# Matmul, GELU, matmul on one core: loads through SyncE's queue with casts on VectorE, and a transpose by the DMA crossbar

## The chip, the core and the metric

The kernel runs on one core of a Trainium2 chip. The core has five engines with instruction streams of their own: TensorE (PE, matrix products; its weight loads are shown apart as PEld), VectorE (DVE), ScalarE (ACT), GpSimd (POOL) and SyncE (SP, which here only issues DMAs). Sixteen DMA engines move data between HBM and the on-chip memory SBUF; PE writes its results to PSUM. The metric is the time of one execution on the device in microseconds (us); less is better.

## The reference

```
a: (1024, 1024)   b: (1024, 2048)   c: (2048, 1024)   all float32
h   = a @ b
h   = 0.5 * h * (1 + tanh(sqrt(2/pi) * (h + 0.044715 * h**3)))
out = h @ c       (1024, 1024) float32
```

## The kernel before

All products run in bf16 with f32 accumulation. A matmul of PE contracts over the 128 partitions, so the first product needs a transposed: `aT[h]` holds half h of a's rows (512 of them) as 8 slices of k. The first product is computed as the transpose of h: for each of the 16 column tiles t of b (128 columns), 8 matmuls over k give a tile of 128 x 512 in PSUM, ACT applies the GELU and writes it to `hT[h]` as bf16 (L103). The second product takes `hT[h]` as it lies: 8 row tiles by 2 column halves, 16 matmuls each (L171), evacuated by DVE (L163) and stored through SP (L164).

The schedule is manual: each engine runs its instructions in the order of the program. The order of the work is this.

- Opening: SP loads half 0 of a and the first 768 columns of b (six tiles, `N0`) as f32, slice of k by slice (L60, L66). DVE casts a (L91), PE transposes it by products with an identity matrix (L94), DVE copies the result from PSUM (L95), ACT casts b (L97). PE runs the six tiles' matmuls k by k, one slice behind (`mm0`, L86).
- A gate on POOL (L75) reads one column of the sixth slice of b, so that POOL's loads start only when that slice has landed.
- All further loads are issued by POOL's queue, which casts f32 to bf16 on the way: the next 512 columns of b (`N1`, four loads of two k slices, L110), the last 768 columns of b (two groups of 384, `W2`, each in two loads of four k slices, L110 too), the second half of a (`ab1`, four loads of 128 rows, L142), then c (eight loads of two tiles, L137).
- PE runs the four tiles of `N1` (L118), then tiles 10 to 15 of half 0 (`mm1(t, 0)`, L127). After tiles 11 to 14 the function `turn(j)` transposes one of the four row blocks of a's second half: eight PE transposes (L149) into one PSUM tile, one copy by DVE into `aT[1]` (L150). Block j fills columns 128 j to 128 j + 127 of each of the eight slices.
- PE then runs all 16 tiles of half 1 (`mm1(t, 1)`, L127), each of which reads all of `aT[1]`, then the second product.

Of the kernel before, what the change touches and what calls it, by code (L numbers as in the profile page):

```python
# [9 lines left out]
F32 = mybir.dt.float32  # L10
BF16 = mybir.dt.bfloat16
# [5 lines left out]
def kernel(ctx, tc, a, b, c, out):  # L17
    nc = tc.nc
    M, K = a.shape
    _, N = b.shape  # L20
    _, P = c.shape
    KT = K // 128
    NT = N // 128
# [7 lines left out]
    av = a.rearrange("(mt p) k -> p mt k", p=128)  # L31
    bv = b.rearrange("(kt p) n -> p kt n", p=128)
    cv = c.rearrange("(nt p) q -> p nt q", p=128)

    ctx.enter_context(tc.manual_schedule())
    consts = ctx.enter_context(tc.tile_pool(name="consts", bufs=1))
    keep = ctx.enter_context(tc.tile_pool(name="keep", bufs=1))
    astage = ctx.enter_context(tc.tile_pool(name="astage", bufs=4))
    abf = ctx.enter_context(tc.tile_pool(name="abf", bufs=4))
    b0stage = ctx.enter_context(tc.tile_pool(name="b0stage", bufs=8))  # L40
    opool = ctx.enter_context(tc.tile_pool(name="opool", bufs=4))
    ppool = ctx.enter_context(tc.tile_pool(name="ppool", bufs=6, space=PSUM))
    tpool = ctx.enter_context(tc.tile_pool(name="tpool", bufs=2, space=PSUM))
# [3 lines left out]
    ident = consts.tile([128, 128], BF16, name="ident")  # L47
    make_identity(nc, ident)

    aT = [keep.tile([128, KT, H], BF16, name=f"aT{h}") for h in range(2)]  # L50
    b_sb = keep.tile([128, KT, N], BF16, name="b_sb")
    c_sb = keep.tile([128, NT, P], BF16, name="c_sb")
# [3 lines left out]
    a_st, b_st = {}, {}  # L56
# [9 lines left out]
        nc.sync.dma_start(out=st, in_=bv[:, k, 0:W0])  # L66
        b_st[k] = st

    gate = consts.tile([128, 1], F32, name="gate")
    for k, n in ((0, 1), (1, 1), (2, 2), (4, 2), (6, 2)):  # L70
        load_a0(k, n)
        for i in range(n):
            load_b0(k + i)

    nc.gpsimd.tensor_copy(gate, b_st[5][:, 0:1])  # L75
    g = consts.tile([128, 1], F32, name="g")
    nc.scalar.activation(g, warm[:, 0:1], AF.Gelu_apprx_tanh)
    wps = tpool.tile([128, H], F32, name="pt")
# [10 lines left out]
    for k in range(KT):  # L89
        ab = abf.tile([128, 4, 128], BF16, name="ab")  # L90
        nc.vector.tensor_copy(ab, a_st[k])  # L91
        pt = tpool.tile([128, H], BF16, name="pt")
# [14 lines left out]


    def load_b(k0, kn, n0, w):
        nc.gpsimd.dma_start(out=b_sb[:, k0:k0 + kn, ds(n0, w)], in_=bv[:, k0:k0 + kn, ds(n0, w)])  # L110

    ps = [(tpool if t < 2 else ppool).tile([128, H], F32, name="pt" if t < 2 else "ps")
          for t in range(N1)]
    for k in range(0, KT, 2):
        load_b(k, 2, W0, W1)
        for i in range(2):
            for t in range(N1):
                nc.tensor.matmul(ps[t], b_sb[:, k + i, ds(W0 + t * 128, 128)], aT[0][:, k + i, :],  # L118
                                 start=(k + i == 0), stop=(k + i == KT - 1))
# [4 lines left out]
    def mm1(t, h):  # L124
        p = ppool.tile([128, H], F32, name="ps")
        for k in range(KT):
            nc.tensor.matmul(p, b_sb[:, k, ts(t, 128)], aT[h][:, k, :],  # L127
                             start=(k == 0), stop=(k == KT - 1))
        gelu(t, h, p)

    W2 = 384
    for n0 in range(W0 + W1, N, W2):
        for k in range(0, KT, 4):
            load_b(k, 4, n0, W2)

    def load_c(t0):
        nc.gpsimd.dma_start(out=c_sb[:, t0:t0 + 2, :], in_=cv[:, t0:t0 + 2, :])  # L137

    a1 = []
    for j in range(4):  # L140
        st = abf.tile([128, K], BF16, name="ab1")
        nc.gpsimd.dma_start(out=st, in_=av[:, 4 + j, :])  # L142
        a1.append(st)

    def turn(j):
        ab = a1[j]
        pt = tpool.tile([128, KT, 128], BF16, name="pt")
        for k in range(KT):
            nc.tensor.transpose(pt[:, k, :], ab[:, ts(k, 128)], ident)  # L149
        nc.vector.tensor_copy(aT[1][:, :, ts(j, 128)], pt)  # L150

    for t in range(N0 + N1, NT):
        mm1(t, 0)
        if NT - 5 <= t < NT - 1:
            turn(t - (NT - 5))
    for t in range(0, NT, 2):
        load_c(t)
    for t in range(NT):
        mm1(t, 1)

# [5 lines left out]
    for mt in range(MT):  # L166
        h, j = divmod(mt, 4)
        for q0, w in ((0, 512), (512, 512)) if mt < MT - 1 else ((0, 512), (512, 256), (768, 256)):
            p = ppool.tile([128, w], F32, name="ps", padded_shape=[128, H])
# [34 lines left out]
```

## Time and profile before

| | us |
|---|---|
| three runs | 133.13, 130.68, 131.53 |
| median | 131.53 |
| the profiled execution | 133.13 |
| its span, first to last instruction | 130.9 |

| engine | busy us | share of the span |
|---|---|---|
| PE | 119.2 | 91% |
| PEld | 56.3 | 43% |
| ACT | 27.2 | 21% |
| DVE | 21.0 | 16% |
| POOL | 14.6 | 11% |

The profiled execution is the slowest of the three, 1.2% above the median. In the lines that follow, L127 is line 127 of the kernel; a group "L149 PE MATMUL pt<-ident,ab" is named by its line, engine, operation, output and inputs. In the 40 slices a digit is an engine's busy share of a slice in tenths. A bracket at the end of a line of the timeline gives the idle time of the engine before the instruction and what ended it.

### The profile page before, as it was taken

To read this page: it belongs to the slowest core of one execution; us is meant where nothing else is said; L and a number is where in the kernel's file an instruction comes from. 1 tells how busy PE (TensorE), PEld (TensorE's weight loads), DVE (VectorE), ACT (ScalarE), POOL (GpSimd) and SP (SyncE) were. 2 spreads that over 40 slices of the span, in tenths; PEclk is the share of its full clock that TensorE was granted. 3 is DMA by queue.
4 is the path that set the end of the run, shared out by engine and by line. 5 is a ranking of instruction groups with operands and counts; after the bars stand their busy time and mean duration, and the time that the engine had idled before them with its cause. 6 is when DMAs were issued, how large, how long until landed. Compare 5 with 4: busy or idle time off the path is not lost.

```text
span 130.9 us, 1420 instructions
## 1 busy us (share of the span) xinstructions
PE 119.2 (91%) x591; PEld 56.3 (43%) x602; DVE 21.0 (16%) x38; ACT 27.2 (21%) x50; POOL 14.6 (11%) x27
## 2 busy tenths in 40 slices
PE   6856899998299999999999999999999999999990
PEld 2323444443155444444444444444444444444570
DVE  0223451000042200000000022222222222211121
ACT  4045556516111333333333100000000000000000
POOL 2000099232462000000000000000000000000000
PEclk9999999999999999999999999999999999999999
DMA  3999999999999999950000022221111222222231
GB/s 110 201 367 380 378 236 168 179 202 205 209 211 210 211 212 211 211 112 1 0 0 0 5 80 80 80 78 59 60 59 69 80 80 80 80 80 80 80 120 40
DMA packets 12196, 17.37 MB, mean 133 GB/s; under 512 B 800, under 2 KB 6688, under 8 KB 12192
## 3 DMA queue, kind: packets, MB, share of 16 engines
q0 software_dynamic: 5952, 7.87, 34.8%
q1 hardware_dynamic: 6240, 9.44, 20.8%
q8 instruction: 4, 0.07, 0.2%
HBM read 20.97 MB, written 4.19 MB: 192 GB/s over the span
## 4 chain that ended last, share of the span: by engine, by line
PE 70%; DMA 18%; POOL 5%; SPq 4%; issue 1%; DVE 0%
PE ps L171 42%; PE ps L127 26%; DMA ab<-in_a_dram 10%; DMA b_st<-in_b_dram 7%; POOL b_sb L110 4%; SPq L66 3%; PE pt L149 1%; SPq L60 1%; DVE ot L163 0%; POOL gate L75 0%
## 5 line engine op out<-in xcount | busy, mean ns | idle before, releaser
L171 PE MATMUL ps<-c_sb,hT 128*128 128x512 bf16 (+1 forms) x267 | 55.2, 367 | 0.3
L127 PE MATMUL ps<-aT,b_sb 128*128 128x512 bf16 x172 | 38.8, 379 | 0.6 <-DMA b_sb<-in_b_dram 0.4
L171 PEld LDWEIGHTS <-hT 128*128 128x128 bf16 x272 | 26.6, 98 | 28.9
L127 PEld LDWEIGHTS <-b_sb 128*128 128x128 bf16 x176 | 16.9, 98 | 20.5 <-DMA b_sb<-in_b_dram 0.9
L103 ACT ACTIVATE hT<-ps 128x512 bf16<-128x512 f32 x30 | 17.3, 602 | 30.0 <-PE ps L127 27.7
L163 DVE COPY ot<-ps 128x512 f32<-128x512 f32 (+1 forms) x17 | 11.2, 660 | 73.2 <-PE ps L171 73.2
L86 PE MATMUL ps<-aT,b_sb 128*128 128x512 bf16 x47 | 11.5, 379 | 0.1
L97 ACT ACTIVATE b_sb<-b_st 128x384 bf16<-128x384 f32 x16 | 7.5, 515 | 10.7 <-DMA b_st<-in_b_dram 10.5
L94 PE MATMUL pt<-ident,ab 128*128 128x128 bf16 x32 | 3.4, 233 | 3.9 <-DVE ab L91 3.9
L137 POOL DMA_DIRECT2D c_sb<-in_c_dram x8 | 5.7, 714 | 6.9 <-DMA b_sb<-in_b_dram 4.7
L86 PEld LDWEIGHTS <-b_sb 128*128 128x128 bf16 x48 | 4.4, 98 | 4.0
L150 DVE COPY aT<-pt 128x1024 bf16<-128x1024 bf16 x4 | 2.8, 692 | 20.5 <-PE pt L149 20.5
L110 POOL DMA_DIRECT2D b_sb<-in_b_dram x8 | 6.0, 775 | 0.0
L80 PE MATMUL pt<-warm 128*128 128x512 bf16 x10 | 4.5, 632 | 1.2 <-DVE warm L46 1.2
L94 PEld LDWEIGHTS <-ab 128*128 128x128 bf16 x32 | 2.3, 104 | 6.9 <-DVE ab L91 5.8
L118 PE MATMUL ps<-aT,b_sb 128*128 128x512 bf16 x16 | 4.8, 379 | 0.1
L118 PEld LDWEIGHTS <-b_sb 128*128 128x128 bf16 x32 | 3.1, 98 | 3.8
L91 DVE CAST ab<-a_st 128x512 bf16<-128x512 f32 x8 | 3.6, 445 | 6.2 <-DMA a_st<-in_a_dram 6.2
L118 PE MATMUL pt<-aT,b_sb 128*128 128x512 bf16 x15 | 4.5, 379 | 0.0
L149 PE MATMUL pt<-ident,ab 128*128 128x128 bf16 x32 | 2.5, 220 | 2.3 <-DMA ab<-in_a_dram 2.3
L95 DVE COPY aT<-pt 128x512 bf16<-128x512 bf16 x8 | 3.4, 425 | 6.4 <-PE pt L94 6.4
L149 PEld LDWEIGHTS <-ab 128*128 128x128 bf16 x32 | 2.0, 98 | 3.5 <-DMA ab<-in_a_dram 2.8
(13 smaller groups left out, 7.5 us busy)
## 6 DMA issues: line engine op xcount, KB each, us to landing
c_sb<-in_c_dram POOLq DMA_DIRECT2D x8, 512.0 KB, 15.3
out_dram<-ot SPq DMA_DIRECT2D x15, 256.0 KB, 2.0
b_st<-in_b_dram SPq DMA_DIRECT2D x8, 384.0 KB, 8.7
a_st<-in_a_dram SPq DMA_DIRECT2D x3, 512.0 KB, 8.9
b_sb<-in_b_dram POOLq DMA_DIRECT2D x4, 384.0 KB, 11.4
b_sb<-in_b_dram POOLq DMA_DIRECT2D x4, 256.0 KB, 5.9
ab<-in_a_dram POOLq DMA_DIRECT2D x4, 256.0 KB, 13.8
a_st<-in_a_dram SPq DMA_DIRECT2D x2, 256.0 KB, 4.2
```

The costliest lines, as they stand in the source:

```text
L80: nc.tensor.matmul(wps, warm[:, 0:128], warm, start=True, stop=True)
L86: nc.tensor.matmul(ps[t], b_sb[:, k, ts(t, 128)], aT[0][:, k, :], start=(k == 0), stop=(k == KT - 1))
L94: nc.tensor.transpose(pt[:, ts(j, 128)], ab[:, j, :], ident)
L97: nc.scalar.activation(b_sb[:, k, ts(i, W0 // 2)], b_st[k][:, ts(i, W0 // 2)], AF.Copy)
L103: nc.scalar.activation(hT[h][:, t, :], p, AF.Gelu_apprx_tanh)
L110: nc.gpsimd.dma_start(out=b_sb[:, k0:k0 + kn, ds(n0, w)], in_=bv[:, k0:k0 + kn, ds(n0, w)])
L118: nc.tensor.matmul(ps[t], b_sb[:, k + i, ds(W0 + t * 128, 128)], aT[0][:, k + i, :], start=(k + i == 0), stop=(k + i == KT - 1))
L127: nc.tensor.matmul(p, b_sb[:, k, ts(t, 128)], aT[h][:, k, :], start=(k == 0), stop=(k == KT - 1))
L137: nc.gpsimd.dma_start(out=c_sb[:, t0:t0 + 2, :], in_=cv[:, t0:t0 + 2, :])
L149: nc.tensor.transpose(pt[:, k, :], ab[:, ts(k, 128)], ident)
L163: nc.vector.tensor_copy(ot[:, 0:w], p)
L171: nc.tensor.matmul(p, hT[h][:, t, ts(j, 128)], c_sb[:, t, ds(q0, w)], start=(t == 0), stop=(t == NT - 1))
```

## The change

The loads that POOL issued with a cast are now issued by SP as f32 into staging buffers and cast by DVE. b and c share a new pool `stage` of three buffers of 8 KB per partition; a's second half goes into the four buffers of the opening's pool `astage`. The gate on POOL is gone. `turn(j)` no longer uses PE, PSUM and DVE's copy, but issues one transposing DMA from the bf16 copy `ab1[j]` into the same columns of `aT[1]`. In the program, and so in SP's queue, the four turns stand after all loads of b and a, with the first four loads of c between them (turn, load of c, turn, load of c, and so on), and the other four loads of c after them; all of this stands ahead of `mm1(10, 0)` in the program. The pool of the opening slices of b, `b0stage`, has eight buffers before and after.

```
+    stage = ctx.enter_context(tc.tile_pool(name="stage", bufs=3))
...
-    gate = consts.tile([128, 1], F32, name="gate")
...
-    nc.gpsimd.tensor_copy(gate, b_st[5][:, 0:1])
...
     def load_b(k0, kn, n0, w):
-        nc.gpsimd.dma_start(out=b_sb[:, k0:k0 + kn, ds(n0, w)], in_=bv[:, k0:k0 + kn, ds(n0, w)])
+        st = stage.tile([128, 2048], F32, name="st")
+        sv = st[:, 0:kn * w].rearrange("p (k n) -> p k n", k=kn)
+        nc.sync.dma_start(out=sv, in_=bv[:, k0:k0 + kn, ds(n0, w)])
+        nc.vector.tensor_copy(b_sb[:, k0:k0 + kn, ds(n0, w)], sv)
...
     def load_c(t0):
-        nc.gpsimd.dma_start(out=c_sb[:, t0:t0 + 2, :], in_=cv[:, t0:t0 + 2, :])
+        st = stage.tile([128, 2048], F32, name="st")
+        sv = st.rearrange("p (t q) -> p t q", t=2)
+        nc.sync.dma_start(out=sv, in_=cv[:, t0:t0 + 2, :])
+        nc.vector.tensor_copy(c_sb[:, t0:t0 + 2, :], sv)
 
     a1 = []
     for j in range(4):
-        st = abf.tile([128, K], BF16, name="ab1")
-        nc.gpsimd.dma_start(out=st, in_=av[:, 4 + j, :])
+        st = astage.tile([128, K], F32, name="a_st")
+        nc.sync.dma_start(out=st, in_=av[:, 4 + j, :])
         a1.append(st)
 
+    ab1 = []
+    for j in range(4):
+        ab = abf.tile([128, K], BF16, name="ab1")
+        nc.vector.tensor_copy(ab, a1[j])
+        ab1.append(ab)
+
     def turn(j):
-        ab = a1[j]
-        pt = tpool.tile([128, KT, 128], BF16, name="pt")
-        for k in range(KT):
-            nc.tensor.transpose(pt[:, k, :], ab[:, ts(k, 128)], ident)
-        nc.vector.tensor_copy(aT[1][:, :, ts(j, 128)], pt)
-
+        nc.sync.dma_start_transpose(out=aT[1][:, :, ts(j, 128)], in_=ab1[j])
+
+    for j in range(4):
+        turn(j)
+        load_c(2 * j)
+    for t in range(8, NT, 2):
+        load_c(t)
     for t in range(N0 + N1, NT):
         mm1(t, 0)
-        if NT - 5 <= t < NT - 1:
-            turn(t - (NT - 5))
-    for t in range(0, NT, 2):
-        load_c(t)
     for t in range(NT):
         mm1(t, 1)
```

## The prediction

> **What bounds the kernel now.** I read the 40 slices of the page first, then the chain of work that ended last in order of time, then the waits of PE, then those of SP's queue.
>
> ```profile
> PE   6856899998299999999999999999999999999990
> DMA  3999999999999999950000022221111222222231
> GB/s 110 201 367 380 378 236 168 179 202 205 209 211 210 211 212 211 211 112 1 0 0 0 5 80 80 80 78 59 60 59 69 80 80 80 80 80 80 80 120 40
> ```
>
> A slice is 3.27 us. PE is full from slice 12 to the end; the only thin places are the opening and slice 11. The DMA engines are full for the first 17 slices, some 57 us: all inputs are fetched once, as fast as the engines go. The GB/s fall to about 205 from slice 7 on because POOL's loads are counted after their cast from f32 to bf16; about 410 GB/s were read.
>
> ```profile
> 16.25 5.83 POOL b_sb L110 x8
> 22.09 13.67 DMA ab<-in_a_dram
> 35.76 0.05 issue
> 35.80 0.62 PE pt L149 x8
> 36.43 0.65 PE ps L127 x3
> ...
> 38.15 0.45 PE pt L149 x8
> ...
> 40.33 0.45 PE pt L149 x8
> ...
> 42.50 0.45 PE pt L149 x8
> 42.95 1.08 PE ps L127 x5
> 44.02 0.05 issue
> 44.08 10.74 PE ps L127 x49
> ```
>
> The columns are start and duration in us. Until 35.8 us the chain runs through the loads, POOL's and then that of the second half of a; from there it is PE alone. The eight matmuls of output tile t = 15 of the first half start with the last transposes done and end at 44.5 us (127 x8 at 0.216 each from 42.78). So **the second half's matmuls start at T = 44.5 us**, and what follows T is fixed: 128 matmuls at 0.2155 us (27.6) and 16 groups of 16 (55.5) to 127.6 us. The whole change is judged by what it does to T. Three lines of the timeline show what PE loses before T:
>
> ```profile
> 30.74 2.27 PEld L127 LDWEIGHTS <-b_sb 128*128 128x128 bf16 x12 [0.90 <-DMA b_sb<-in_b_dram]
> 30.75 2.76 PE L127 MATMUL ps<-aT,b_sb 128*128 128x512 bf16 x12 [0.41 <-DMA b_sb<-in_b_dram]
> 35.80 0.62 PE L149 MATMUL pt<-ident,ab 128*128 128x128 bf16 x8 [2.29 <-DMA ab<-in_a_dram]
> ```
>
> It waits 0.4 us for b and 2.3 us for a; the four transpose groups take 0.62 + 3 x 0.45 = 2.0 us. That is 4.7 us, so T cannot fall below 39.8 us.
>
> **What the Trainium skill says.** "DMA: Bandwidth & Descriptors", section "Queues, rings and completion order": all that SP issues goes to one ring on each DMA engine, and a ring's descriptors are consumed in order. The trace agrees: the opening's loads of a, all issued by SP, need 2.6 us to land at the shortest and 9.9 at the longest, and loads of a and b land in the order of issue. "VectorE: DVE Perf Modes", section "The three transpose paths": a 128x128 bf16 transpose takes 1309 ns through the DMA crossbar and 390 on TensorE. The trace has 220 ns for a PE transpose and eight in 0.45 us; it has no crossbar transpose. "TensorE: Matmul & The Clock Gate", section "What's actually happening": after an idle window of about 3.4 us PE runs at half rate until it has been busy for about as long. The trace shows the slow start: the ten warm-up matmuls of L80 take 4.45 us, and the same shape later needs 0.216 each.
>
> **The change, part by part.**
>
> *Loads move from POOL to SP, without cast.* SP's order is now the opening (5.24 MB), four loads of b of 0.524 MB, four of 0.786, four of a of 0.524, then turn 0, c 0, turn 1, c 2, turn 2, c 4, turn 3, c 6 (1.05 MB each c), then the rest of c. Bytes read are the same. From HBM in f32, SP's loads ran at 367 to 380 GB/s in slices 3 to 5; I take 380, against about 410 for POOL's. Slices 1 to 5 hold 4.70 MB by 16.36 us, so the opening's last byte moves at 17.8; the last a slice's landing (17.5 us by its cast, at 4.46 MB) gives a lag of some 1.6 us from movement to landing. The gate on POOL goes: it kept the other loads behind the opening, and the order of SP's ring does that now. I cost it at nothing; if the ring did not keep order, the opening would lose up to 1.4 us for each load that overtakes.
>
> *Casts go to DVE.* By the Trainium skill's "VectorE: DVE Perf Modes", section "The perf-mode tier table (the rule you actually need)" (2048 f32 elements from SBUF in 1227 ns; the trace's 445 ns for 512 fits the same slope, 0.52 ns an element) I estimate 0.69 us for 1024 elements, 0.96 for 1536 and 1.23 for 2048: 4 x 0.69 + 4 x 0.96 + 4 x 0.69 + 8 x 1.23 = 19.2 us in all, less four copies of 0.69 (L150). DVE is otherwise idle from 20.4 to 75 us, so this hides, but each cast adds to the way of its load, and DVE keeps order.
>
> *Three stage buffers.* SP's fourth load waits for the first cast, and behind it in SP's order wait the loads of a and the turns. My walk: loads 1 to 3 of b land at 20.8, 22.2, 23.5; cast 1 ends at 21.5 (DVE's last opening copy ends at 20.4), load 4 lands at 25.0, loads 5 to 8 at 27.2, 29.3, 31.4, 33.5, casts a microsecond later. PE wants slice pairs of b at 22.4, 24.1, 25.8, 27.6, tiles 10 to 12 at 29.3 (second half of k at 30.15; cast 30.2), tiles 13 to 15 at 34.5. All hold to within 0.1 us, so PE finishes the first half at 39.8, and the 0.4 us wait for b is gone. With no bubble the 12.58 MB up to the last a would have moved by 37.1 us; my walk gives 37.5. a lands at 34.9, 36.3, 37.6, 39.0, and its last cast ends at 39.7.
>
> *Transposes leave PE.* PE saves 2.0 us and DVE four copies. Each turn moves 0.262 MB from SBUF to SBUF. Bounds: the skill's "DMA: Bandwidth & Descriptors", section "Latency and other measured facts" gives 261 GB/s for transposing, so 1.0 us; eight blocks at 1309 ns one after the other are 10.5 us. The trace's nearest row, a plain DMA, is 0.7 us for so many bytes. I take 1.5 us on the DMA engines, near the lower end, because the 1309 ns of a lone block must be mostly fixed latency.
>
> *Turns and c loads share SP's ring.* The first matmul of the second half needs all four turns (each fills 128 of 512 columns). Turn 0 can be issued at 35.6 (cast 0), but moves behind the last a, at 37.5. Then three c loads of 1.05 MB, 2.75 us each, lie ahead of turn 3. So **turn 3 has moved at 37.5 + 4 x 1.5 + 3 x 2.75 = 51.8 us and landed at 53.4**. That is the new T. In the kernel before no load of c stood ahead of the matmuls in this way: c followed a in POOL's queue. If SP stays held while a transpose runs, each c load is issued only afterwards and some 1 us more is lost per pair, at most 3.
>
> *PE idles* from 39.8 to 53.4, far over the idle window, so it restarts at half rate. The warm-up's 4.2 us at half rate would lose 2.1, the page's 3.4 us 1.7; I take 1.9 (0 to 2.1).
>
> *c on time?* After turn 3 five c loads remain, 13.8 us of movement, landed and cast by about 69 us; the second product starts near 83. Nothing there, nor in the stores, which come later on SP. PSUM loses only the transpose tiles' use.
>
> **Sum.** T moves by 53.4 - 44.5 = +8.9 us, the cold restart adds 1.9: **+10.8 us**. The profiled execution took 133.13 us, 130.9 of span and 2.2 around it; it was 1.6 above the median of 131.53. So 143.9 for that execution and **142.3 us** against the median. The low end of this case (400 GB/s, turns of 1.0 us, no bubble and no cold restart) has T at 49.6 and 136.6 us; the high end (SP held, turns of 2 us) has T at 58.4 and 147 to 148.
>
> **Rivals.**
>
> *The turns do not wait for c (not slower).* If transposes overtake queued copies or the c loads are issued too late to stand in front, turn 3 starts when cast 3 ends, at 39.7, and needs what the first load of a needed, 2.7 us from issue to landing, plus 0.3 to 0.8 for its longer movement: T = 42.7 to 43.2, -1.8 to -1.3 us, 129.7 to 130.2 us. A wholly hidden transpose would give T = 39.8 and 126.8 us. The deciding point: one c load ahead of turn 3 puts T at 45.5, still within 2%, two at 48.2 with PE cold, which is not. For it speaks only that SP's second c load might be held up; against it, that buffers for c 0, 2 and 4 are free (loads 6, 7, 8 of b are cast by 34.5) and that the ring keeps order.
>
> *The transposes are slow (slower still).* If a turn takes 4 us and SP is held, with the ring drained around each, the three pairs take 3 x (4 + 3.9), then 4 and the landing: T = 66.8, so 131.5 + 22.3 + 1.9 = 155.7 us. At 10.5 us a turn it would be some 180. For it: the lone-block price; against it, the page's rate of 261 GB/s.
>
> *It does not do what it says.* Of more buffers for b's opening slices the diff shows nothing: they have eight already. If the turn were written element by element instead of through the crossbar, that is the slow rival's far end.
>
> **How the numbers follow.** The queue case 0.66, the slow transposes 0.20, the overtaking or hidden ones 0.10, something slower that I don't see, such as the three buffers starving PE in the first half, 0.04. The range of 135.5 to 154 leaves out the overtaking case and the slow one's tail, under 2 in 10. About 2% (128.9 to 134.2) is what a measurement can tell from no change: slower by more 0.87, within 0.09 (overtaking at 129.7 lies here), faster 0.04 (fully hidden only).
>
> **What would show it.** Right: PE idle some 12 us before the first matmul of the second half, released by a DMA into aT; the fourth transpose's landing after c loads; half-rate matmuls after it; PE full from then on; no wait on b over 1 us between 22 and 40 us. Wrong: transposes landing near 43 us with c still queued, a turn of over 3 us on its own, or PE waiting for casts of b before 39 us.

## The result, and the profile after

The changed kernel takes **142.02 us** (median of four runs, 141.3 to 144.09) against 131.11 us for the kernel before in the same comparison: 1.083 times the time, with a 95% interval of 1.072 to 1.095. Ratios here and below compare fast runs alone (executions over 1.5% above the fastest of their kernel stay out), so they can differ a little from the ratio of the medians given. The prediction was 142.3 us, slower. The profiled execution took 141.3 us with a span of 139.4.

First the 40 slices of the page, now 3.49 us wide:

```profile
PE   6789999969960029999999999999999999999990
PEclk9999999999998556999999999999999999999999
DMA  4999997999999999992000002222212122222221
```

PE has a hole in slices 13 and 14, and the clock granted to it (PEclk) falls to half there and right behind it. The DMA engines have none: the loads run on through the hole. The chain that ended last says what PE waits for (start, duration, what):

```profile
37.53 5.77 DMA st<-in_c_dram
43.31 0.02 issue
43.33 0.76 DVE c_sb L142
44.09 7.11 DMA aT<-ab
51.20 0.14 issue
51.34 8.04 PE ps L129 x29
```

The fourth turn is issued by SP at 44.09 us and lands 7.1 us later; the second half of the first product starts at **T = 51.34 us**. (The step over DVE's cast is only the inference of the releaser: SP was busy issuing c 4 until 44.0.) SP's own timeline shows what it puts into its ring (start, time for which it holds SP, what):

```profile
36.14 1.35 SPq L157 DMA_TRANSPOSE aT<-ab  x1
37.53 0.60 SPq L141 DMA_DIRECT2D st<-in_c_dram  x1
38.24 1.24 SPq L157 DMA_TRANSPOSE aT<-ab  x1
39.52 0.65 SPq L141 DMA_DIRECT2D st<-in_c_dram  x1
40.27 3.08 SPq L157 DMA_TRANSPOSE aT<-ab  x1
43.40 0.59 SPq L141 DMA_DIRECT2D st<-in_c_dram  x1
44.09 2.83 SPq L157 DMA_TRANSPOSE aT<-ab  x1
```

and DVE's casts of c, each of which starts when its load has landed, show when the ring delivers:

```profile
43.33 1.23 DVE L142 CAST c_sb<-st 128x2048 bf16<-128x2048 f32 x1 [3.39 <-DMA st<-in_c_dram]
46.94 1.23 DVE L142 CAST c_sb<-st 128x2048 bf16<-128x2048 f32 x1 [2.39 <-DMA st<-in_c_dram]
50.39 1.23 DVE L142 CAST c_sb<-st 128x2048 bf16<-128x2048 f32 x1 [2.22 <-DMA st<-in_c_dram]
53.83 1.23 DVE L142 CAST c_sb<-st 128x2048 bf16<-128x2048 f32 x1 [2.21 <-DMA st<-in_c_dram]
56.51 1.23 DVE L142 CAST c_sb<-st 128x2048 bf16<-128x2048 f32 x1 [1.46 <-DMA st<-in_c_dram]
59.05 1.23 DVE L142 CAST c_sb<-st 128x2048 bf16<-128x2048 f32 x1 [1.31 <-DMA st<-in_c_dram]
```

c 0, 2 and 4 land at 43.3, 46.9 and 50.4 us, and turn 3 at 51.2, right behind the third. Where a turn lies between two loads of c they are 3.4 to 3.6 us apart, later 2.5 to 2.7: a load of c takes about 2.55 us, a turn about 0.9 to 1.05. The landings of the turns (their last semaphore updates in the trace) agree: 40.2, 44.3, 47.8 and 51.2 us, each 0.8 to 1.0 us after the load that lies before it in the queue.

Two of PE's stretches behind the hole (window, length, busy us and matmuls started per engine, clock, DMA share, GB/s):

```profile
51.40:54.60 3.20, 3.20 (x8) 1.11 (x9) 0.99 (x2) 0.00 (x0) 0.00 (x0) 0.50 1.03 410
54.60:57.80 3.20, 3.20 (x16) 1.46 (x15) 1.68 (x2) 1.19 (x2) 0.00 (x0) 0.99 1.03 410
```

Eight matmuls at half rate, then 16 in the same time. From T to the end of the span it is 88.0 us.

The shown profile of the kernel before is of an execution of 133.13 us. A second one, of an execution of 131.67 us (span 129.6), was expected like this:

> The kernel before once more, for a second profile: the shown one comes from the slowest of its executions (133.13 us against a median of 131.1 to 132.0). If only the opening differs between executions, the second half starts up to 2 us earlier than 44.5 us, with the same 86.4 us after it.

Its timeline:

```profile
40.99 0.61 PE L149 MATMUL pt<-ident,ab 128*128 128x128 bf16 x8
41.43 6.86 PE L127 MATMUL ps<-aT,b_sb 128*128 128x512 bf16 x31
```

The first eight of these matmuls belong to tile 15 of the first half (1.72 us), so T, read as in the prediction, is 43.2 us there, 1.3 earlier than in the shown execution, with the same 86.4 us after it. Only what comes before T differs. Between this profile and that of the changed kernel the change costs 51.3 - 43.2 = 8.2 us at T (from unrounded times) and 88.0 - 86.4 = 1.6 behind it: 9.8 us, the difference of the spans.

### The profile page after: what moved, and what is told of

It reads as the page before. It is cut to its first block, busy times and chain, and to the rows that moved or that the text cites. A ratio compares the mean times of both kernels' runs of the same rounds, so it can differ in the third digit from the quotient of the medians.

```text
span 139.4 us, 1384 instructions
## 1 busy us (share of the span) xinstructions
PE 120.5 (86%) x560; PEld 55.4 (40%) x570; DVE 37.2 (27%) x54; ACT 27.2 (20%) x50; POOL 0.7 (1%) x6
## 4 chain that ended last, share of the span: by engine, by line
PE 61%; DMA 31%; SPq 3%; DVE 3%; issue 1%
PE ps L179 39%; PE ps L129 21%; DMA st<-in_b_dram 11%; DMA b_st<-in_b_dram 6%; DMA aT<-ab 5%; DMA a_st<-in_a_dram 5%; DMA st<-in_c_dram 4%; DVE b_sb L112 1%; SPq L67 1%; SPq L61 1%; DVE c_sb L142 1%; DVE ab L153 1%; SPq L147 0%; DVE ot L171 0%; SPq L111 0%
## 5 line engine op out<-in xcount | busy, mean ns | idle before, releaser
L129 PE MATMUL ps<-aT,b_sb 128*128 128x512 bf16 x173 | 40.0, 390 | 12.1 <-DMA aT<-ab 10.7
L129 PEld LDWEIGHTS <-b_sb 128*128 128x128 bf16 x176 | 17.3, 100 | 34.7 <-issue 13.4
L102 ACT ACTIVATE hT<-ps 128x512 bf16<-128x512 f32 x30 | 17.3, 601 | 39.2 <-PE ps L129 37.0
L142 DVE CAST c_sb<-st 128x2048 bf16<-128x2048 f32 x8 | 9.8, 1227 | 17.0 <-DMA st<-in_c_dram 17.0
L85 PE MATMUL ps<-aT,b_sb 128*128 128x512 bf16 x47 | 12.7, 410 | 0.1
L112 DVE CAST b_sb<-st 128x1024 bf16<-128x1024 f32 (+1 forms) x8 | 6.6, 827 | 8.8 <-DMA st<-in_b_dram 8.8
L85 PEld LDWEIGHTS <-b_sb 128*128 128x128 bf16 x48 | 4.7, 104 | 4.7 <-issue 1.1
L93 PE MATMUL pt<-ident,ab 128*128 128x128 bf16 x32 | 3.6, 243 | 1.9 <-DVE ab L90 1.9
L120 PE MATMUL ps<-aT,b_sb 128*128 128x512 bf16 x16 | 4.8, 379 | 0.1
L120 PEld LDWEIGHTS <-b_sb 128*128 128x128 bf16 x32 | 3.1, 98 | 3.8
L93 PEld LDWEIGHTS <-ab 128*128 128x128 bf16 x32 | 2.5, 108 | 5.0 <-DVE ab L90 3.7
L153 DVE CAST ab<-a_st 128x1024 bf16<-128x1024 f32 x4 | 2.8, 694 | 2.1 <-DMA a_st<-in_a_dram 2.1
L79 PEld LDWEIGHTS <-warm 128*128 128x128 bf16 x10 | 1.3, 144 | 3.4 <-issue 2.2
L102 ACT ACTIVATE hT<-pt 128x512 bf16<-128x512 f32 x2 | 1.1, 594 | 4.3 <-PE pt L120 4.3
```

What stands on the lines that cost most here:

```text
L79: nc.tensor.matmul(wps, warm[:, 0:128], warm, start=True, stop=True)
L85: nc.tensor.matmul(ps[t], b_sb[:, k, ts(t, 128)], aT[0][:, k, :], start=(k == 0), stop=(k == KT - 1))
L93: nc.tensor.transpose(pt[:, ts(j, 128)], ab[:, j, :], ident)
L102: nc.scalar.activation(hT[h][:, t, :], p, AF.Gelu_apprx_tanh)
L112: nc.vector.tensor_copy(b_sb[:, k0:k0 + kn, ds(n0, w)], sv)
L142: nc.vector.tensor_copy(c_sb[:, t0:t0 + 2, :], sv)
```

## The experiments

Ratios are to the kernel before, run beside each group on the same chip (131.7 to 132.0 us).

**No load of c ahead of the turns.**

```
     for j in range(4):
         turn(j)
-        load_c(2 * j)
-    for t in range(8, NT, 2):
+    for t in range(0, NT, 2):
         load_c(t)
```

> The four turns are issued before the first load of c; everything else as in the changed kernel. Theory (the turns queue behind three loads of c in SP's ring): turn 3 is issued at about 40 us, when the last a is cast, and lands near 43; PE's gap before the second half shrinks from 10.7 to about 2.5 us, too short for a restart at half rate, so 142.0 - 8.3 - 1.7 = 132 us, the kernel before (131.1) within 2%. Rival (a crossbar transpose is slow by itself, some 3 us each with SP held): the turns still end near 50 us and the time stays at 139 to 142 us.

Measured: 134.16 us, ratio 1.020 (1.011 to 1.028). Two lines of its timeline:

```profile
36.82 5.75 SPq L157 DMA_TRANSPOSE aT<-ab  x4
44.57 21.79 PE L129 MATMUL ps<-aT,b_sb 128*128 128x512 bf16 x91 [4.02 <-DMA aT<-ab]
```

The four turns are through SP in 5.75 us, and T falls from 51.3 to 44.6. So 6.8 of the 8.2 us come from the three loads of c alone. T is 1.5 us later than expected (the last a landed 0.7 us later in this execution than in that of the changed kernel), the gap is 4.0 us, not 2.5, and PE still restarts at half rate; so 132 was missed by two.

**One load of c ahead.** The loop keeps `load_c(0)` after turn 0; the rest of c follows turn 3.

```
     for j in range(4):
         turn(j)
-        load_c(2 * j)
-    for t in range(8, NT, 2):
+        if j == 0:
+            load_c(0)
+    for t in range(2, NT, 2):
         load_c(t)
```

> One load of c (after turn 0) stands ahead of turn 3 instead of three; the others follow turn 3. Theory (ring order; 2.6 us for each c load ahead, 0.9 for each turn): c 0 lands near 43.3 us as in the changed kernel, turns 1 to 3 0.9 us apart behind it, so the second half starts at 46.0 us and the time is 142.0 - 5.3 = 136.7 us. Rival (no order in the ring; SP's holding of a turn and the landing time of each turn make the loss, whatever stands ahead): 134 us as with no c ahead, or 142 as with three.

Measured: 137.33 us, ratio 1.044 (1.039 to 1.050), T at 47.5:

```profile
47.49 18.81 PE L129 MATMUL ps<-aT,b_sb 128*128 128x512 bf16 x73 [6.40 <-DMA aT<-ab]
```

This is 1.5 us later than expected, 1.0 of it because the last a landed later in this execution (40.2 us). T is 44.6, 47.5 and 51.3 us with none, one and three loads of c ahead: it follows what stands ahead in the ring, and neither value of the rival came.

**Each turn twice.**

```
+    aX = keep.tile([128, KT, H], BF16, name="aX")
...
     def turn(j):
+        nc.sync.dma_start_transpose(out=aX[:, :, ts(j, 128)], in_=ab1[j])
         nc.sync.dma_start_transpose(out=aT[1][:, :, ts(j, 128)], in_=ab1[j])
```

> The changed kernel with each turn issued twice, the first time into a spare tile that nobody reads. It measures what a turn itself takes in the ring. Theory (0.9 us of movement a turn): four more turns ahead of the second half put it at 51.3 + 3.6 = 54.9 us, 145.6 us. Prediction's value (1.5 us): 148 us. Rival (turns run one after the other with some 3 us each): 154 us.

Measured: 150.85 us, T at 59.6:

```profile
59.64 6.55 PE L129 MATMUL ps<-aT,b_sb 128*128 128x512 bf16 x19 [18.80 <-DMA aT<-ab]
```

Four more turns cost 8.3 us at T, 2.1 each, more than any of my values but the rival's 3. The landings in the trace show that the turns themselves did not take that long. A turn directly behind another landed 0.8 to 0.9 us after it, as the theory had it: 3.5 us for the four. Most of the rest, 4.3 us, is in the three loads of c ahead of the last turns, which landed 4.6, 3.9 and 4.0 us after the turn before them instead of 3.1, 2.6 and 2.6 in the changed kernel. They were issued later. SP is held for 4.1 us by the second turn of a pair and issues c 2 only at 45.6 us, when c 0 has all but landed (45.8); in the changed kernel c 2 is issued at 39.5 and c 0 lands at 43.3. That the late issue is the whole of the 4.3 us is likely but was not tried.

**PE kept busy in the hole.**

```
         mm1(t, 0)
+    wps = tpool.tile([128, H], F32, name="pt")
+    for _ in range(48):
+        nc.tensor.matmul(wps, warm[:, 0:128], warm, start=True, stop=True)
     for t in range(NT):
```

> The changed kernel with 48 matmuls of zeros (10.3 us) between the two halves of the first product, where PE idles 10.7 us. Theory (1.7 us of the loss is a restart at half rate): the second half starts at the same 51.3 us but at full rate, 142.0 - 1.7 = 140.3 us. Rival (the slow matmuls after the gap have another cause, or the modelled clock is an artefact): 142.0 us, and slow matmuls after the gap as before.

Measured: 140.41 us against 142.02 for the changed kernel. The PE timeline of the profiled execution (141.03 us):

```profile
40.53 10.52 PE L168 MATMUL pt<-warm 128*128 128x512 bf16 x47
52.70 1.67 PE L129 MATMUL ps<-aT,b_sb 128*128 128x512 bf16 x7 [1.65 <-DMA aT<-ab]
```

T is 1.4 us later in this execution, where the theory had it unchanged, so the times alone do not price the restart. From T to the end it is 139.1 - 52.7 = 86.4 us instead of 88.0: the restart at half rate cost 1.6 us, where the theory had 1.7.

**PE's turns with SP's loads.** `turn` is that of the kernel before, reading `ab1[j]`; c follows the last turn.

```
     def turn(j):
-        nc.sync.dma_start_transpose(out=aT[1][:, :, ts(j, 128)], in_=ab1[j])
-
-    for j in range(4):
-        turn(j)
-        load_c(2 * j)
-    for t in range(8, NT, 2):
-        load_c(t)
+        ab = ab1[j]
+        pt = tpool.tile([128, KT, 128], BF16, name="pt")
+        for k in range(KT):
+            nc.tensor.transpose(pt[:, k, :], ab[:, ts(k, 128)], ident)
+        nc.vector.tensor_copy(aT[1][:, :, ts(j, 128)], pt)
...
         mm1(t, 0)
+        if NT - 5 <= t < NT - 1:
+            turn(t - (NT - 5))
+    for t in range(0, NT, 2):
+        load_c(t)
```

> Loads by SP with casts on DVE as in the changed kernel, but the turns on PE after tiles 11 to 14 with a copy by DVE, and c after them, as in the kernel before. Theory: the new way of loading costs nothing by itself; the last a is cast at 40 us, PE's turns add 2.0 us, the second half starts near 43 us and the time is 130 to 132 us. Rival (SP's queue, three stage buffers and DVE's casts are what costs): it stays over 136 us.

Measured: 134.36 us, ratio 1.021 (1.010 to 1.031): neither what the theory nor what the rival said. Its timeline:

```profile
31.15 2.76 PE L129 MATMUL ps<-aT,b_sb 128*128 128x512 bf16 x12 [1.08 <-DVE b_sb L112]
35.61 0.69 DVE L153 CAST ab<-a_st 128x1024 bf16<-128x1024 f32 x1 [0.34 <-DMA a_st<-in_a_dram]
36.36 0.62 PE L160 MATMUL pt<-ident,ab 128*128 128x128 bf16 x8 [2.45 <-DVE ab L153]
```

PE waits 1.1 us for a cast of b and 2.45 for that of a, and T is 45.1 us. In the second run of the kernel before PE's first turn starts at 34.45 us, here at 36.36. So loading by SP with casts is not free: it brings the second half of a 1.9 us later to PE. The cast on DVE is 0.7 of that. The other 1.2 is a later landing (35.6 us against 34.4 by the traces); whether the three buffers or the rate of SP's loads make it was not tried.

**The turns by DMA, all loads by POOL.** The kernel before with this alone:

```
     def turn(j):
-        ab = a1[j]
-        pt = tpool.tile([128, KT, 128], BF16, name="pt")
-        for k in range(KT):
-            nc.tensor.transpose(pt[:, k, :], ab[:, ts(k, 128)], ident)
-        nc.vector.tensor_copy(aT[1][:, :, ts(j, 128)], pt)
+        nc.sync.dma_start_transpose(out=aT[1][:, :, ts(j, 128)], in_=a1[j])
+    for j in range(4):
+        turn(j)
     for t in range(N0 + N1, NT):
         mm1(t, 0)
-        if NT - 5 <= t < NT - 1:
-            turn(t - (NT - 5))
```

> The kernel before with nothing changed but the turns: transposing DMAs on SP, whose ring holds nothing else then, while c comes through POOL's queue. Theory: the last a lands at 39.8 us as in the kernel before, turn 3 lands some 3 to 4 us later even though c is moving, the second half starts at 43 to 44.5 us: 129.5 to 131.5 us. Rival (a transpose beside loads of c is slow whatever the queue): second half at 49 us or later, 136 us or more.

Measured: 154.51 us, ratio 1.176 (1.165 to 1.187), far from the theory; it is what the rival said, and goes far beyond its bound of 136. SP's ring holds nothing but the turns, yet its timeline shows turns 1 and 2 holding SP for

```profile
36.89 10.51 SPq L146 DMA_TRANSPOSE aT<-ab  x1
...
47.49 11.50 SPq L146 DMA_TRANSPOSE aT<-ab  x1
```

and T is 64.2 us, after the last of c:

```profile
64.23 11.03 PE L127 MATMUL ps<-aT,b_sb 128*128 128x512 bf16 x38 [24.13 <-DMA aT<-ab]
```

Turn 0 lands at 51.6 us and turn 1 at 62.5, 10.8 us apart; c has landed at 62.3, and turns 2 and 3 follow 0.8 and 0.9 us apart. Nothing in the program makes a turn wait for c; the two only share the DMA engines. The page counts 4224 more packets under 512 B than in the kernel before, 1056 a turn, 66 for each engine. c's rows are 4 KB each, 0.16 us at 410/16 GB/s. If an engine takes one packet of each ring in turn, a turn lasts 66 x 0.16 = 10.6 us. That is what the Trainium skill says in "DMA: Bandwidth & Descriptors", section "Queues, rings and completion order": an engine goes round the queues that have work, packet by packet. Counted from the trace's packet records, 16 engines together:

```
                     packets   packets of    of these,   mean us of
                     of turns  POOL's queue  data of c   one of c
40 to 42 us            177         178          174         0.175
44 to 46 us            191         191          176         0.172
```

One for one, if the 4-byte writes with which a load ends are counted too; the counts do not show the order within a stretch. Two further kernels test it.

```
     def load_c(t0):
-        nc.gpsimd.dma_start(out=c_sb[:, t0:t0 + 2, :], in_=cv[:, t0:t0 + 2, :])
+        for q in (0, 512):
+            nc.gpsimd.dma_start(out=c_sb[:, t0:t0 + 2, ds(q, 512)], in_=cv[:, t0:t0 + 2, ds(q, 512)])
```

> The kernel with POOL's loads and DMA turns (154.5 us) with each load of c cut into two of 512 columns, so that a packet reads 2 KB instead of 4 and there are twice as many. Theory (the engines alternate packet by packet between SP's ring and POOL's, so a turn of 66 packets per engine takes 66 x 0.16 = 10.6 us beside 4 KB packets): beside 2 KB packets a turn takes 5.3 us, the second half starts near 54 us instead of 64.2, and the time is about 144 us. Rival (a turn simply waits until c is through): 154 us again.

Measured: 156.53 us, so the expected time is missed and the rival's is nearer. The turns themselves did what the theory said; SP is held for

```profile
36.51 5.53 SPq L147 DMA_TRANSPOSE aT<-ab  x1
42.14 7.01 SPq L147 DMA_TRANSPOSE aT<-ab  x1
49.24 6.22 SPq L147 DMA_TRANSPOSE aT<-ab  x1
```

about 6 us a turn instead of 11, and the turns land 6.3 to 6.5 us apart. (By the packet records a packet of c takes 0.096 us here, not 0.08: 66 x 0.096 = 6.3.) What my sum forgot: c has twice the packets now, 4096, about as many as the four turns, and they alternate to the end of c. Before, c had 2048 packets and left the last turns a free road. The sum over all stays:

```profile
65.62 0.61 PE L127 MATMUL ps<-aT,b_sb 128*128 128x512 bf16 x1 [25.93 <-DMA aT<-ab]
```

The other kernel holds c back until turn 3 has landed:

```
+    gate2 = consts.tile([128, 1], BF16, name="gate2")
+    nc.gpsimd.tensor_copy(gate2, aT[1][:, KT - 1, H - 1:H])
     for t in range(0, NT, 2):
         load_c(t)
```

> The kernel with POOL's loads and DMA turns (154.5 us), but POOL's loads of c wait for turn 3 to land. Theory (there the turns were starved by c's packets on the other ring, each of some 66 packets per DMA engine waiting for one of c's): with c away the turns land as with SP's loads, 3.2 us after issue, so that the second half starts at 43 to 44 us; 130.5 to 133 us, with up to 1.7 us of restart at half rate in it. Rival (a turn behind POOL's loads is slow for another reason, such as POOL's descriptors or the cast): over 140 us. c, 21 us of movement, is there by 66 us, before the second product either way.

Measured: 134.27 us, ratio 1.013 (1.006 to 1.020), T at 42.9:

```profile
42.89 23.41 PE L127 MATMUL ps<-aT,b_sb 128*128 128x512 bf16 x93 [3.34 <-DMA aT<-ab]
```

With c away, turn 3 lands 3.2 us after its issue and 20 us are gained. The time is 1.3 us above the upper end expected, mostly because PE's restart costs 2.7 us here, not 1.7 (below).

**Two versions that aim below the kernel before.** One only moves PE's turns:

```
-        if NT - 5 <= t < NT - 1:
-            turn(t - (NT - 5))
+        for j in {12: (0,), 13: (1,), 14: (2, 3)}.get(t, ()):
+            turn(j)
```

> The kernel before with PE's turns placed later: turn 0 after tile 12, turn 1 after 13, turns 2 and 3 after 14, so that PE doesn't wait 2.3 us for the second half of a after tile 11. Expected: the second half starts 1.7 us earlier, some 130.0 us against 131.7. Rival (what PE saves there it waits later for the last a, which lands at 39.8 us, or for DVE's copy): 131.7 us.

Measured: 129.84 us, ratio **0.985** (0.980 to 0.990). Its timeline:

```profile
34.65 0.62 PE L149 MATMUL pt<-ident,ab 128*128 128x128 bf16 x8 [0.41 <-DMA ab<-in_a_dram]
...
39.01 1.06 PE L149 MATMUL pt<-ident,ab 128*128 128x128 bf16 x16
...
39.90 8.37 PE L127 MATMUL ps<-aT,b_sb 128*128 128x512 bf16 x38
```

PE's wait for a is 0.4 us instead of 1.9 in the second run of the kernel before, and T, eight matmuls after 39.90, is 41.6, 1.5 us earlier. The other version uses the crossbar where it has time: it is the kernel with c held back, with turns 0 to 2 by DMA, turn 3 by PE and c waiting for turn 2.

```
-    for j in range(4):
+    for j in range(3):
         turn(j)
     for t in range(N0 + N1, NT):
         mm1(t, 0)
+    pt = tpool.tile([128, KT, 128], BF16, name="pt")
+    for k in range(KT):
+        nc.tensor.transpose(pt[:, k, :], a1[3][:, ts(k, 128)], ident)
+    nc.vector.tensor_copy(aT[1][:, :, ts(3, 128)], pt)
...
-    nc.gpsimd.tensor_copy(gate2, aT[1][:, KT - 1, H - 1:H])
+    nc.gpsimd.tensor_copy(gate2, aT[1][:, KT - 1, 383:384])
```

> POOL's loads, turns 0 to 2 by DMA on SP, turn 3 by PE after tile 15, and c on POOL's queue held until turn 2 has landed. Expected: turn 2 is issued at 38.3 us and lands at 41.5, PE's turn with its copy is done by then, PE's gap is too short for half rate; the second half starts at 41.6 us, some 2.5 us better than the kernel before: 129 us. Rival (turns behind one another land later, or PE is slowed again): 131 us or more.

Measured: 130.9 us, ratio 0.988 (0.983 to 0.993), T at 42.2:

```profile
39.87 0.61 PE L154 MATMUL pt<-ident,ab 128*128 128x128 bf16 x8
40.52 0.69 DVE L155 COPY aT<-pt 128x1024 bf16<-128x1024 bf16 x1 [19.88 <-PE pt L154]
...
42.18 5.99 PE L127 MATMUL ps<-aT,b_sb 128*128 128x512 bf16 x27 [1.70 <-DMA aT<-ab]
```

PE's turn 3 was copied by 41.2, and PE still waited for turn 2 on the crossbar, which landed at 42.05, not 41.5. So the expected 129 was missed and the rival's 131 is nearer, though PE was not slowed. Both versions come out 1.2 to 1.5% below the kernel before, with intervals that leave out 1 but less than the 2% that the prediction counted as a change; between the two the intervals overlap.

## Why the prediction was right

- **The turns queue behind c in SP's ring.** Shown: taking the loads of c away from ahead of the turns gives back 6.8 us of T, one of them puts T in between, and turn 3 lands 0.8 us behind c 4 in the changed kernel.
- **T at 53.4 us.** It was 51.3. The last a landed as expected (39.2; 39.0 predicted), but by two errors that cancel: by the packet records it had moved at 38.7 us, not 37.5, and landed 0.5 us later, not 1.6. Behind it the three loads of c took 3.1, 2.6 and 2.6 us from landing to landing, 8.3 in all, as predicted. The four turns took 3.7 us (0.8 to 1.0 each), not 6.0: this term is the error of T. The skill's 261 GB/s (1.0 us) was the better price here. What the upper end feared, SP held while a transpose runs, came in part: turns 2 and 3 held SP for 3.1 and 2.8 us. It cost little, because c 4 was still issued 3.5 us before c 2 had landed and the DMA row has no gap; in the doubled kernel, where the loads of c were issued later, they landed 4.3 us later.
- **Restart at half rate, 1.9 us.** 1.6 by the kernel with PE kept busy. In other runs it came to as much as 2.7 (below), beyond the 2.1 that was allowed for.
- **T at 44.5 us before.** True of the shown execution only; the second profile has 43.2. The sum of +10.8 us stands against 9.8 between the profiles and 10.9 between the medians: the error in the turns and that in the start partly cancel, and the closeness of 142.3 to 142.02 is better than the working.
- **Loads and casts cost nothing on the path.** Wrong, but covered. The changed kernel's timeline:

```profile
28.88 1.04 PE L129 MATMUL ps<-aT,b_sb 128*128 128x512 bf16 x4 [0.19 <-DVE b_sb L112]
30.95 9.67 PE L129 MATMUL ps<-aT,b_sb 128*128 128x512 bf16 x43 [1.03 <-DVE b_sb L112]
```

PE waited 0.2 and 1.0 us for casts of b, where at most 0.1 was expected: load 6's cast ended at 30.9 us, not 30.2. The prediction had named such a wait, before 39 us, as a sign that it was wrong. The first half then ended at 40.6, ten microseconds before the turns were there. With PE's turns the same loads cost 2%.

- **The overtaking rival** rested on the turns not standing behind c. In a ring of their own they don't, and are slower still, which neither rival had: they then share each engine packet by packet with c. Its deciding point was set too low as well: one load of c ahead was to give T at 45.5 and a time within 2%, and gave 47.5 and 4.4%. The slow rival's price of 4 us a turn was nowhere near for a turn alone and far too low beside another ring.

## What to carry to other kernels

A transfer that something waits for belongs ahead of bulk loads in its queue: look at the order of issue and at how many bytes lie before it. Moving it to a queue of its own did not help here, where it is made of small packets and the other queue had large ones; holding the bulk back until it had landed did. And an engine relieved of 2 us of work gains next to nothing if its replacement needs 3 us from issue to landing at the very point where the engine waits: with c held back, T was 42.9 us against 43.2, and the restart cost more than that.

## What was not expected of the hardware

Beside 4 KB packets of another ring, transposes of 0.26 MB landed 10.8 us apart and held SP for 10.5 to 11.5; beside 2 KB packets they landed 6.3 to 6.5 apart and held it for 5.5 to 7.0; between loads of its own ring one took about 1.

PE's restart does not grow with the gap. Times in us; "half clock" is how long after T the trace's record of the granted clock still stands at half:

```
kernel                      PE's gap   half clock  T to the second  T to
                            before T   after T     product          the end
before, second run             0          0            27.6          86.4
PE kept busy                   1.7        0            27.6          86.4
three turns DMA, one PE        1.7        0            27.6          86.7
c held back                    3.3        5.6          30.4          89.5
no c ahead                     4.0        3.2          29.2          87.9
one c ahead                    6.4        5.5          30.3          89.1
changed kernel                10.7        3.3          29.2          88.0
turns doubled                 18.8        4.7          29.9          88.8
DMA turns, POOL's loads       24.1        5.0          30.1          89.2
the same, c in halves         25.9        3.4          29.3          88.4
```

A gap of 1.7 us costs the first product nothing, one of 3.3 us or more costs it 1.6 to 2.7 (from unrounded times), in no order of length. In every row the loss is, to 0.1 us, half of the time under "half clock". The half-clock stretches that hold these restarts last 3.41, 6.83, 10.24, 20.48, 23.89 and 27.31 us in the clock records, whole multiples of 3.41. So what counts is where T falls in such a stretch, and not how long PE was idle. This fits the Trainium skill's "TensorE: Matmul & The Clock Gate", section "What's actually happening", where the window that is watched, about 3.4 us long, runs freely and the end of the slow phase depends on where in it the work starts. The page has PE slowed after an idle window of about 3.4 us; here less was enough, for with c held back the clock record falls to half 2.1 us after PE's last matmul, in a gap of 3.3. The measurement decides: gaps of 3.3 us and more were slowed in these runs, gaps of 1.7 were not.
